# Shift and scale in three parts, and the order of the first sums, at the start of a pool and state-space decoder layer

## The chip, the cores and the metric

The kernel runs on one core of a Trainium2 chip. A core has a matrix engine (TensorE, PE in the profile), a vector engine (VectorE, DVE), a scalar engine with activation functions (ScalarE, ACT), a general engine (GpSimd, POOL), a queue engine that issues most transfers (SyncE, SP), and 16 DMA engines that move data between the chip's memory (HBM) and the core's two on-chip memories: SBUF, 128 partitions wide, and PSUM, into which PE writes.

The metric is the time of one execution on the device in microseconds (us), smaller is better. Of the kernel before there are three timed runs and one profiled execution, whose trace gives the start, the duration and the waits of every instruction.

## The reference

One layer for 1,024 prompt tokens and 64 sample tokens (8 sequences of 8), so 1,088 columns in all, with 1,024 features. Cut to what matters here:

```python
mod = jax.nn.silu(c) @ w_ada + b_ada
shift, scale, gate = jnp.split(mod, 3, axis=-1)
h = rmsnorm(x, norm_g) * (1 + scale[:, None]) + shift[:, None]
proj = h @ w_in
u_pool, z_pool, z_ssm, xbc, dt_raw, g_raw = jnp.split(proj, SPLITS, axis=-1)
...
dt = jax.nn.softplus(dt_raw + dt_bias)
...
gates = jax.nn.sigmoid(g_raw)
m = gates[..., :D_MODEL] * p + gates[..., D_MODEL:] * s
x = x + gate[:, None] * (m @ w_o)
```

`c` has nine rows: one for the prompt, eight for the samples. So shift, scale and gate are nine rows of 1,024 numbers each, made with a 1,024 x 3,072 matrix. All is in 32-bit floats.

## The kernel before

All products are made of two halves of the numbers: `hi`, which PE takes at its fast rate, and `lo`, the rest (number minus `hi`). A product is three matmuls: high by high, low by high, high by low. Activations stand with the features on the partitions, in eight blocks of 128 called k. Most of the later products with `w_in` are done two output blocks at a time by a scheme with seven products in place of eight (`strassen`, L561-623), which needs sums and differences of the four quarters of h (`combine`, L440-488) and of the weights (`first_steps`, L516).

The change lies in `first()` (L819-972), which begins the program. Its instructions are held in the order in which they are written, on each engine (`in_line`, L300); what follows is ordered by a scheduler. Its steps:

- `x_load`, `x_square`, `x_root`, `x_unit` (L207-211): nine blocks of 128 tokens (the ninth has 64) are loaded, their root mean square is made, and each is divided by it. Blocks 5 and 6 are scaled on POOL, the others on DVE.
- `x_turn(g, k)` (L215-228): PE turns feature block k of token group g (256, 384 and 448 tokens: x-blocks 0-1, 2-4, 5-8) by transposes, then a copy to `tf[k]`, for even k on DVE and for odd k on ACT.
- `ada_load`, `ada_mm`, `ada_end` (L235-259): the columns of `w_ada` for shift and scale in two parts of half the features each, eight loads of 512 KB a part. A step `ada_mm(part, k)` has four matmuls of 256 columns, each into its own 32 partitions of one PSUM bank. `ada_end` copies the bank on ACT (`mr`, L249), turns it back with two transposes (L252) and makes `md`, the scale and shift by feature, with three operations on DVE (L256, L259, L256).
- `h_make(g, ks)` (L269-295): for each k, ACT makes the high half straight from `tf` (L283, for the group with samples L292), ACT (odd k) or DVE (even k) makes h itself in place (L285, L287), and DVE the low half by subtraction (L275). Only k with `md` ready can be done, so the first half of the features comes first.
- `w_load`, `w_split` (L825 and below): the weights of two output blocks of `g_raw`, 256 KB for each half of the features, are loaded and split into `whi` (ACT, L160) and `wlo` (POOL or, where asked, DVE, L163).
- `products(g, ks)` (L837-850): these weights by h, six matmuls for each k and token group. `done` (L854-858) applies the sigmoid on ACT and stores it.
- `dt_block` (L691): the 32 columns of dt. Its activation (L701) writes into a buffer that earlier sigmoids used and that must have been stored.
- `gate_load`, `gate_mm` (L800), `gate_end` (L813): the third part of `mod`.
- `combine()` is a generator; each `next(sums)` does one portion. The first four portions are for k = 0, 1, 2 and 3: three additions or subtractions on DVE (L466-468) over half of the tokens (544 columns), the high half of `S2` on ACT (L469) and, one k behind, its low half on DVE (L462). The next portion makes `S3` (ACT L446, DVE L447, four times), then come `S1` (a subtraction, L481, high and low) and the last operand. Here `next` is called four times up to the opening and up to five times in it.
- `next(wst)` does one portion of the differences and splits of the weights of the seven products.
- `late_loads()` (L332-347) loads small constants; its second portion copies `dx` (L342, DVE) and turns two tiles on PE (L344, L345) and copies the results (L346, L347). The opening's products stand behind L345 in PE's order.
- the opening, `run(wz, hook)`: the seven products of the first two output blocks of z, 24 matmuls of 272 columns each. `hook(n)` is called behind product n and does portions of the weights (`wst`) and of the sums.

The calls ahead of the opening:

Of the kernel before, what the change touches and what calls it, by code (L numbers as in the profile page):

```python
# [8 lines left out]
F32 = mybir.dt.float32  # L9
F32R = mybir.dt.float32r  # L10
AF = mybir.ActivationFunctionType
ALU = mybir.AluOpType
# [8 lines left out]
P = 128  # L21
D = 1024
KT = D // P
# [23 lines left out]
def tile_pool_ssd_step(  # L47
# [6 lines left out]
    nc = tc.nc  # L54
# [25 lines left out]
    hp = open_("hp", 8)  # L80
# [6 lines left out]
    def G(shape=(P, T), dt=F32):  # L87
        return hp.tile(list(shape), dt, tag="G", name=nm("G"), bufs=8)
# [4 lines left out]
    def Y4(pool, dt=F32R):  # L93
        return pool.tile([P, 4, T], dt, tag="Y", name=nm("Y"), bufs=2)
# [87 lines left out]
    xr = []  # L182
# [24 lines left out]
    def x_unit(a, b):  # L207
        n = xr[a][1]
        V.reciprocal(rs[:n, a:b], rs[:n, a:b])
        for i in range(a, b):  # L210
            (nc.gpsimd if i in (5, 6) else V).tensor_scalar(xr[i][0][:n], xr[i][0][:n], rs[:n, i:i + 1], None, ALU.mult)

    tf = [None] * KT

    def x_turn(g3, k, eng=None):  # L215
        if g3 == 0:
            tf[k] = tfp.tile([P, T], F32, tag="tf", name=nm("tf"), bufs=8)
        px = PB()
        c = 0
        for i in range((0, *XG)[g3], XG[g3]):  # L220
            xt, n = xr[i]
            nc.tensor.transpose(px[:, c:c + n], xt[:n, k * P:(k + 1) * P], ident[:n, :n])
# [8 lines left out]
    pm, wraw = [None] * 2, {}  # L231
    wbig = [Y4(hp, F32), Y4(hp, F32)]
    md = const([P, 16, 9], "md")

    def ada_load(part, k):  # L235
        w = wbig[k // 4][:, k % 4, :D] if part == 0 else G((P, D))
        wraw[part, k] = w.rearrange("p (s c) -> p s c", s=2)
        load(wraw[part, k], w_ada[0, k * P:(k + 1) * P, 0:2 * D].rearrange("p (s h c) -> p s h c", s=2, h=2)[:, :, part])

    def ada_mm(part, k):  # L240
        if k == 0:
            pm[part] = PB()
        for j in range(4):
            mm(pm[part][32 * j:32 * j + 32, :256], scT[:, k, :], wraw[part, k][:, j // 2, j % 2 * 256:j % 2 * 256 + 256],
               start=(k == 0), stop=(k == KT - 1))

    def ada_end(part):
        mr = pa.tile([P, 256], F32, tag="rawA", name=nm("mr"), bufs=3)
        act(mr, pm[part][:, :256], AF.Copy)  # L249
        ps = PB()  # L250
        for i in range(2):
            nc.tensor.transpose(ps[:, i * P:(i + 1) * P], mr[:, i * P:(i + 1) * P], ident)  # L252
        pv = ps[:, :256].rearrange("p (i j b) -> p j i b", i=2, j=4)
        for s in (1, 0):
            m4 = slice(8 * s + 4 * part, 8 * s + 4 * part + 4)
            V.tensor_tensor(md[:, m4].rearrange("p (j i) b -> p j i b", i=2), pv[:, 2 * s:2 * s + 2, :, 0:9],  # L256
                            vT[:, m4].rearrange("p (j i) -> p j i", i=2).unsqueeze(3).to_broadcast([P, 2, 2, 9]), ALU.add)
            if s:
                V.tensor_tensor(md[:, m4], md[:, m4],  # L259
                                vT[:, 16 + 4 * part:20 + 4 * part].unsqueeze(2).to_broadcast([P, 4, 9]), ALU.mult)  # L260

    hb = []

# [68 lines left out]
    def late_loads():  # L332
        va = sm.tile([120, P], F32, tag="stc", name="va", bufs=4)
        load(va[0:96, :], conv_w[0].rearrange("k (m p) -> (k m) p", p=P))
        load(va[96:120, :], conv_b[0].rearrange("(m p) -> m p", p=P))
        V.memset(dtb, 0.0)
        load(dtb[0:NH, 0:1], dt_bias[0].rearrange("(h o) -> h o", o=1))
        dk = sm.tile([16, 2], F32, tag="rsm", name="dk")
        load(dk, d_skip[0].rearrange("(m h) -> m h", h=2))
        yield  # L340
        dx = sm.tile([16, 2, 64], F32, tag="stc", name="dx", bufs=4)
        V.tensor_copy(dx, dk.unsqueeze(2).to_broadcast([16, 2, 64]))  # L342
        ps = PB()
        nc.tensor.transpose(ps[:, :120], va, ident[:120, :120])  # L344
        nc.tensor.transpose(ps[:, 120:136], dx.rearrange("m h r -> m (h r)"), ident[:16, :16])  # L345
        V.tensor_copy(cvT, ps[:, :120])  # L346
        V.tensor_copy(Dv, ps[:, 120:136])  # L347
# [471 lines left out]
    def first():  # L819
# [34 lines left out]
        def done(bi, t):  # L854
            o, n = BLK[bi]
            buf = pa.tile([P, HF], F32, tag=next(tags), name=nm("g0"))
            act(buf[:, :n], banks[bi, t], AF.Sigmoid)
            store_(gs_d[t][:, o:o + n], buf[:, :n])
# [1029 lines left out]
```

## Time and profile before

| | us |
|---|---|
| timed runs: median (lowest to highest) | 1302.08 (1297.84 to 1302.78) |
| the profiled execution, its own time | 1303.16 |
| its span, first to last instruction | 1301.4 |
| mean granted clock of PE in it, share of full speed | 0.99 |
| first product (L848) starts | 39.65 |
| second half of h (k 4 to 7) starts on ACT | 57.25 |
| opening's first product (L568) starts | 84.24 |

A row of the profile names the engine, the line of the kernel, the operation, `out<-in` by the program's names, the shape and the count. Brackets at the end give the time that the engine was idle ahead of it and what ended that. In sums by stretch, each engine's busy time and count is followed by PEclk, the clock that PE was granted (1.00 is full), the busy share of the DMA engines (which can show a little over 1), and GB/s.

### The profile page before, as it was taken

What the parts mean: (1) busy time and instruction counts of PE and PEld (TensorE: products, weight loads), DVE (VectorE), ACT (ScalarE), POOL (GpSimd) and SP (SyncE); (2) the same over time, 40 slices, a digit from 0 to 9 for tenths busy, and PEclk for the clock granted to TensorE, in tenths of its full rate; (3) what the DMA queues carried; (4) which work ended last, traced back from release to release, by engine and by line L of the source; (5) the groups of instructions that cost most, each with busy time, mean ns of one, the idle gap of its engine ahead of it and who ended that gap; (6) DMA issues with size and microseconds to landing.
All of it is one profiled execution on the core that took longest, in us unless ns stands there. A gap on an engine that the chain in (4) does not pass through costs nothing.

```text
span 1301.4 us, 26116 instructions
## 1 busy us (share of the span) xinstructions
PE 1260.4 (97%) x9603; PEld 1162.7 (89%) x9603; DVE 888.8 (68%) x1507; ACT 698.3 (54%) x1659; POOL 681.0 (52%) x564
## 2 busy tenths in 40 slices
PE   5999999999999999999999999999999999999998
PEld 3778999999999999998889899888889888999786
DVE  4677579966979588775757665477666777476433
ACT  4665347465656654545555554676887866201211
POOL 2005659778869776664344453366676646214000
PEclk8999999999999999999999999999999999999999
DMA  9735445465456554444546465999998665475631
GB/s 325 231 127 177 149 147 175 149 198 188 138 168 211 157 169 133 160 134 128 166 145 196 148 176 166 351 361 372 296 280 279 210 187 163 164 273 158 228 103 51
DMA packets 231616, 251.66 MB, mean 193 GB/s; under 512 B 31137, under 2 KB 173681, under 8 KB 231482
## 3 DMA queue, kind: packets, MB, share of 16 engines
q1 hardware_dynamic: 159392, 171.59, 41.6%
q10 hardware_dynamic: 72098, 78.41, 17.7%
q8 instruction: 76, 1.25, 0.4%
q14 instruction: 50, 0.41, 0.1%
HBM read 167.06 MB, written 83.01 MB: 192 GB/s over the span
## 4 chain that ended last, share of the span: by engine, by line
PE 54%; issue 8%; POOL 5%; DMA 5%; DVE 4%; ACT 3%; SPq 0%; ACTq 0%; POOLq 0%; DVEq 0%
PE ps L568 5%; PE ps L569 5%; PE ps L570 5%; PE mm L568 5%; PE mm L570 5%; PE mm L569 5%; PE mm L320 3%; PE mm L321 3%; PE mm L322 3%; PE ps L1834 2%; PE ps L1835 2%; PE ps L1836 2%; PE ps L1160 1%; POOL G L1743 1%; PE ps L1376 1%
## 5 line engine op out<-in xcount | busy, mean ns | idle before, releaser
L163 POOL TENSOR_TENSOR wlo<-rawA,whi 128x512 fp32r<-128x512 f32 x120 | 184.0, 1538 | 188.8 <-ACT whi L160 108.1
L163 POOL TENSOR_TENSOR wlo<-raw,whi 128x512 fp32r<-128x512 f32 x92 | 149.9, 1636 | 103.7 <-ACT whi L160 98.0
L320 PE MATMUL mm<-Y,whi 128*128 128x352 f32 (+1 forms) x480 | 163.8, 341 | 0.7 <-DVE G L1737 0.6
L321 PE MATMUL mm<-Y,whi 128*128 128x352 f32 (+1 forms) x480 | 157.9, 329 | 1.0 <-DVE Y L1411 1.0
L322 PE MATMUL mm<-Y,wlo 128*128 128x352 f32 (+1 forms) x480 | 157.2, 328 | 0.0
L568 PE MATMUL mm<-Y,whi 128*128 128x272 f32 x496 | 146.4, 295 | 0.7 <-DVE u L579 0.4
L568 PE MATMUL ps<-Y,whi 128*128 128x272 f32 x496 | 144.5, 291 | 1.5 <-ACT o L768 0.8
L570 PE MATMUL mm<-Y,wlo 128*128 128x272 f32 x496 | 143.1, 289 | 2.1 <-POOL wlo L163 2.1
L569 PE MATMUL mm<-Y,whi 128*128 128x272 f32 x496 | 143.1, 289 | 0.4 <-DVE Y L447 0.4
L569 PE MATMUL ps<-Y,whi 128*128 128x272 f32 x496 | 143.1, 289 | 0.0
L570 PE MATMUL ps<-Y,wlo 128*128 128x272 f32 x496 | 142.7, 288 | 0.0
L1003 DVE SCALAR_TENSOR_TENSOR GA<-GA,cvT,GA 128x1112 f32<-128x1112 f32 x72 | 128.4, 1787 | 0.1
L160 ACT ACTIVATE whi<-rawA 128x512 fp32r<-128x512 f32 x125 | 78.1, 626 | 93.1 <-PE ps L569 38.5
L160 ACT ACTIVATE whi<-raw 128x512 fp32r<-128x512 f32 x96 | 58.8, 626 | 86.7 <-DVE raw L514 43.2
L320 PEld LDWEIGHTS mm<-Y,whi 128*128 128x128 f32 x480 | 90.7, 189 | 6.5 <-issue 3.8
L570 PEld LDWEIGHTS mm<-Y,wlo 128*128 128x128 f32 x496 | 93.4, 188 | 3.0 <-POOL wlo L163 2.7
L568 PEld LDWEIGHTS ps<-Y,whi 128*128 128x128 f32 x496 | 93.4, 188 | 3.0 <-ACT o L768 1.0
L568 PEld LDWEIGHTS mm<-Y,whi 128*128 128x128 f32 x496 | 93.3, 188 | 2.8 <-issue 0.8
L569 PEld LDWEIGHTS mm<-Y,whi 128*128 128x128 f32 x496 | 93.4, 188 | 1.5 <-DVE Y L447 0.8
L569 PEld LDWEIGHTS ps<-Y,whi 128*128 128x128 f32 x496 | 93.3, 188 | 0.4 <-issue 0.2
L570 PEld LDWEIGHTS ps<-Y,wlo 128*128 128x128 f32 x496 | 93.4, 188 | 0.2 <-issue 0.2
L321 PEld LDWEIGHTS mm<-Y,whi 128*128 128x128 f32 x480 | 90.7, 189 | 1.7 <-DVE Y L1411 1.6
(446 smaller groups left out, 3789.0 us busy)
## 6 DMA issues: line engine op xcount, KB each, us to landing
rawA<-in_w_in SPq DMA_DIRECT2D x46, 512.0 KB
dec<-acs_d SPq DMA_DIRECT2D x32, 512.0 KB
xbc<-GA ACTq DMA_DIRECT2D x24, 512.0 KB
xb<-xbc SPq DMA_DIRECT2D x32, 384.0 KB
rawA<-in_w_in SPq DMA_DIRECT2D x32, 256.0 KB
pw<-in_w_ssm_out ACTq DMA_DIRECT2D x32, 256.0 KB
ws<-ph ACTq DMA_DIRECT2D x32, 256.0 KB
ws<-pw SPq DMA_DIRECT2D x32, 256.0 KB
```

Source lines behind the costliest of these rows:

```text
L160: ins = act(hi[:, :, :ncols], raw[:, :, :ncols], AF.Copy)
L163: (eng or nc.gpsimd).tensor_tensor(lo[:, :, :ncols], raw[:, :, :ncols], hi[:, :, :ncols].bitcast(F32), ALU.subtract)
L320: mm(ps[:, :n], a, rh[k][:, o:o + n], start=(k == 0), stop=False)
L321: mm(ps[:, :n], a, rl[k][:, o:o + n], start=False, stop=False)
L322: mm(ps[:, :n], b, rh[k][:, o:o + n], start=False, stop=(k == nk - 1))
L568: mm(p, hi, ah, start=(k == 0), stop=False)
L569: mm(p, hi, al, start=False, stop=False)
L570: mm(p, lo, ah, start=False, stop=(k == 3))
L1003: V.scalar_tensor_tensor(d[:, :n], rp[:, k:k + n], cvT[:, 24 * k + mc:24 * k + mc + 1], d[:, :n], ALU.mult, ALU.add)
L1834: mm(ps[:, :cw], mhk, wo[k][0][:, s], start=(k == 0), stop=False)
L1835: mm(ps[:, :cw], mhk, wo[k][1][:, s], start=False, stop=False)
L1836: mm(ps[:, :cw], mlk, wo[k][0][:, s], start=False, stop=(k == 7))
```

## The change

`first()` and its helpers are changed in five ways:

1. Block 5 is scaled on DVE and block 6 on ACT. The turns (2,4) and (2,5) are both copied on ACT.
2. Shift and scale are made in three parts: k 0-1, k 2-3 and k 4-7. A load of the first two parts has 256 KB, its step four matmuls of 128 columns; the last part is as each part was before. Copy, transposes and the three operations are done once a part (`ada_out`, `ada_end`).
3. h and products follow in three rounds: k 0-1, 2-3, 4-7. The turns (2,6) and (2,7) come behind the first products. The loads for the second half of the weights of g, the last four loads of shift and scale and the first portion of `late_loads` are issued behind the second part's steps.
4. The first three portions of `combine` stand between the sigmoids, two sigmoids and a portion for each token group; then two dt blocks, the portion with the fourth sum, the first splits of weights, the third dt block, and the portion that makes `S3`; the second portion of `late_loads` follows that.
5. In the opening, portions of the sums are done behind products 0, 1, 3 and 4, of the weights behind 0, 2, 3 and 4.

```diff
         for i in range(a, b):
-            (nc.gpsimd if i in (5, 6) else V).tensor_scalar(xr[i][0][:n], xr[i][0][:n], rs[:n, i:i + 1], None, ALU.mult)
+            xt = xr[i][0][:n]
+            if i == 6:
+                act(xt, xt, AF.Copy, scale=rs[:n, i:i + 1])
+            else:
+                V.tensor_scalar(xt, xt, rs[:n, i:i + 1], None, ALU.mult)
...
-        if eng is not V and k % 2:
+        if eng is not V and (eng or k % 2):
...
+    PARTS = ((0, 2), (2, 4), (4, 8))
...
     def ada_load(part, k):
-        w = wbig[k // 4][:, k % 4, :D] if part == 0 else G((P, D))
-        wraw[part, k] = w.rearrange("p (s c) -> p s c", s=2)
-        load(wraw[part, k], w_ada[0, k * P:(k + 1) * P, 0:2 * D].rearrange("p (s h c) -> p s h c", s=2, h=2)[:, :, part])
+        a, b = PARTS[part]
+        w = (b - a) * P
+        if part == 0:
+            if k == 0:
+                wtile[0] = Y4(hp, F32)
+            t = wtile[0][:, k // 2, k % 2 * 512:k % 2 * 512 + 2 * w]
+        elif part == 1:
+            if k % 2 == 0:
+                wtile[1, k // 2] = G((P, D))
+            t = wtile[1, k // 2][:, k % 2 * 512:k % 2 * 512 + 2 * w]
+        else:
+            t = G((P, D))
+        wraw[part, k] = t.rearrange("p (s c) -> p s c", s=2)
+        load(wraw[part, k], w_ada[0, k * P:(k + 1) * P, 0:2 * D].rearrange("p (s c) -> p s c", s=2)[:, :, a * P:b * P])
...
     def ada_mm(part, k):
+        a, b = PARTS[part]
+        n = (b - a) * P // 2
...
-            mm(pm[part][32 * j:32 * j + 32, :256], scT[:, k, :], wraw[part, k][:, j // 2, j % 2 * 256:j % 2 * 256 + 256],
+            mm(pm[part][32 * j:32 * j + 32, :n], scT[:, k, :], wraw[part, k][:, j // 2, j % 2 * n:j % 2 * n + n],
...
+    def ada_out(part):
+        a, b = PARTS[part]
+        n = (b - a) * P // 2
         mr = pa.tile([P, 256], F32, tag="rawA", name=nm("mr"), bufs=3)
-        act(mr, pm[part][:, :256], AF.Copy)
+        act(mr[:, :n], pm[part][:, :n], AF.Copy)
+        return mr
...
         for k in range(KT):
-            if k == 2:
-                w_load(0, 1)
-                w_load(1, 1)
             ada_load(1, k)
+        for k in range(4):
+            ada_load(2, k)
         late = late_loads()
-        next(late)
...
-        ada_mm(0, 0)
         for k in range(4):
-            x_turn(2, k)
-            if k % 2:
-                ada_mm(0, 1 + k // 2)
+            ada_mm(0, k)
+        x_turn(2, 0)
+        x_turn(2, 1)
+        ada_mm(0, 4)
+        ada_mm(0, 5)
         w_split(0, 0)
         w_split(1, 0)
-        ada_mm(0, 3)
-        x_turn(2, 4)
-        ada_mm(0, 4)
-        x_turn(2, 5)
-        ada_mm(0, 5)
+        x_turn(2, 2)
+        x_turn(2, 3)
         ada_mm(0, 6)
         ada_mm(0, 7)
+        mr = ada_out(0)
+        x_turn(2, 4, nc.scalar)
+        x_turn(2, 5, nc.scalar)
+        ada_end(0, mr)
+
+        h_make(0, range(2))
+        products(0, range(2))
         x_turn(2, 6)
-        ada_end(0)
-
-        h_make(0, range(4))
         x_turn(2, 7)
-        products(0, range(4))
-        h_make(1, range(4))
-        ada_mm(1, 0)
-        ada_mm(1, 1)
+        h_make(1, range(2))
+        products(1, range(2))
+        h_make(2, range(2))
+        for k in range(KT):
+            ada_mm(1, k)
+        w_load(0, 1)
+        w_load(1, 1)
+        for k in range(4, 8):
+            ada_load(2, k)
+        next(late)
+        mr = ada_out(1)
+        products(2, range(1))
+        ada_end(1, mr)
+        products(2, range(1, 2))
+
+        for bi in range(2):
+            h_make(bi, range(2, 4))
+            products(bi, range(2, 4))
+        h_make(2, range(2, 4))
         w_split(0, 1, V)
         w_split(1, 1, V)
-        products(1, range(4))
-        h_make(2, range(4))
-        for k in range(2, 8):
-            ada_mm(1, k)
-        products(2, range(2))
+        for k in range(4):
+            ada_mm(2, k)
+        products(2, range(2, 3))
+        for k in range(4, 8):
+            ada_mm(2, k)
+        mr = ada_out(2)
+        products(2, range(3, 4))
...
         next(wst)
-        ada_end(1)
-        products(2, range(2, 4))
+        ada_end(2, mr)
...
+        sums = combine()
+        for bi in range(3):
+            done(bi, 0)
+            done(bi, 1)
+            next(sums)
+        dt_block(dtw, 0)
+        dt_block(dtw, 1)
+        next(sums)
         next(wst)
-        for bi in range(3):
-            for t in range(2):
-                done(bi, t)
-        sums = combine()
-        for i in range(3):
-            dt_block(dtw, i)
-            next(sums)
+        dt_block(dtw, 2)
+        next(sums)
         for k in range(4, 8):
             gate_mm(k)
         next(late, None)
-        next(sums)
         gate_end(bg)
-        next(wst)

         def hook(n):
-            if 0 < n < 4:
+            if n in (0, 2):
                 next(wst)
-            if n < 5:
+            if n < 2:
+                next(sums)
+            if n in (3, 4):
+                next(wst)
                 next(sums)
         run(wz, hook)
```

More of the change, by code (lines that the diff above doesn't have):

```diff
@@ L228, in x_turn @@
             V.tensor_copy(tf[k][:, o:o + c], px[:, :c])
-    pm, wraw = [None] * 2, {}
-    wbig = [Y4(hp, F32), Y4(hp, F32)]
+    PARTS = ((0, 2), (2, 4), (4, 8))
+    pm, wraw, wtile = [None] * 3, {}, {}
     md = const([P, 16, 9], "md")
     def ada_load(part, k):
-        w = wbig[k // 4][:, k % 4, :D] if part == 0 else G((P, D))
-        wraw[part, k] = w.rearrange("p (s c) -> p s c", s=2)
-        load(wraw[part, k], w_ada[0, k * P:(k + 1) * P, 0:2 * D].rearrange("p (s h c) -> p s h c", s=2, h=2)[:, :, part])
+        a, b = PARTS[part]
[12 more added lines that the diff above has]
+        load(wraw[part, k], w_ada[0, k * P:(k + 1) * P, 0:2 * D].rearrange("p (s c) -> p s c", s=2)[:, :, a * P:b * P])
     def ada_mm(part, k):
+        a, b = PARTS[part]
+        n = (b - a) * P // 2
         if k == 0:
@@ L243, in ada_mm, with ada_end @@
         for j in range(4):
-            mm(pm[part][32 * j:32 * j + 32, :256], scT[:, k, :], wraw[part, k][:, j // 2, j % 2 * 256:j % 2 * 256 + 256],
+            mm(pm[part][32 * j:32 * j + 32, :n], scT[:, k, :], wraw[part, k][:, j // 2, j % 2 * n:j % 2 * n + n],
                start=(k == 0), stop=(k == KT - 1))
-    def ada_end(part):
+    def ada_out(part):
+        a, b = PARTS[part]
+        n = (b - a) * P // 2
         mr = pa.tile([P, 256], F32, tag="rawA", name=nm("mr"), bufs=3)
-        act(mr, pm[part][:, :256], AF.Copy)
+        act(mr[:, :n], pm[part][:, :n], AF.Copy)
+        return mr
+    def ada_end(part, mr):
+        a, b = PARTS[part]
+        ni = (b - a) // 2
         ps = PB()
-        for i in range(2):
+        for i in range(ni):
             nc.tensor.transpose(ps[:, i * P:(i + 1) * P], mr[:, i * P:(i + 1) * P], ident)
-        pv = ps[:, :256].rearrange("p (i j b) -> p j i b", i=2, j=4)
+        pv = ps[:, :ni * P].rearrange("p (i j b) -> p j i b", i=ni, j=4)
         for s in (1, 0):
-            m4 = slice(8 * s + 4 * part, 8 * s + 4 * part + 4)
-            V.tensor_tensor(md[:, m4].rearrange("p (j i) b -> p j i b", i=2), pv[:, 2 * s:2 * s + 2, :, 0:9],
-                            vT[:, m4].rearrange("p (j i) -> p j i", i=2).unsqueeze(3).to_broadcast([P, 2, 2, 9]), ALU.add)
+            m = slice(8 * s + a, 8 * s + b)
+            V.tensor_tensor(md[:, m].rearrange("p (j i) b -> p j i b", i=ni), pv[:, 2 * s:2 * s + 2, :, 0:9],
+                            vT[:, m].rearrange("p (j i) -> p j i", i=ni).unsqueeze(3).to_broadcast([P, 2, ni, 9]), ALU.add)
             if s:
-                V.tensor_tensor(md[:, m4], md[:, m4],
-                                vT[:, 16 + 4 * part:20 + 4 * part].unsqueeze(2).to_broadcast([P, 4, 9]), ALU.mult)
+                V.tensor_tensor(md[:, m], md[:, m],
+                                vT[:, 16 + a:16 + b].unsqueeze(2).to_broadcast([P, b - a, 9]), ALU.mult)
     hb = []
```

## The prediction

> **What bounds the kernel now.** I read the page first, then the sums over two stretches of the span (windows: busy time of each engine, granted PE clock, share of the DMA engines, GB/s), and then went through the first stretch with the timeline of each engine and the waits of PE.
>
> ```profile
> span 1301.4 us, 26116 instructions
> PE 1260.4 (97%) x9603; PEld 1162.7 (89%) x9603; DVE 888.8 (68%) x1507; ACT 698.3 (54%) x1659; POOL 681.0 (52%) x564
> 0.00:112.00 112.00, 92.96 (x713) 72.07 (x713) 75.49 (x154) 64.02 (x117) 15.79 (x36) 0.92 0.64 212
> 112.00:1301.40 1189.40, 1167.41 (x8893) 1090.64 (x8891) 813.36 (x1354) 634.31 (x1543) 665.16 (x528) 1.00 0.59 192
> 20.00:30.00 10.00, 5.69 (x30) 2.79 (x31) 3.42 (x8) 1.50 (x4) 5.37 (x2) 0.58 1.07 367
> ```
>
> PE sets the end. After 112 us it is busy for 1167.41 of 1189.40 us at full clock. Nothing there changes its order, so what is gained or lost before 112 us is carried to the end about one for one. Before that PE is idle for 19 us and the granted clock averages 0.92: that is all the change can work on. Three places matter: the wait on GpSimd's two blocks, the chain from the last shift/scale matmul to the first product, and the wait ahead of the opening.
>
> ```profile
> 19.15 6.22 POOL L211 TENSOR_SCALAR Y<-Y,rs 128x1024 f32<-128x1024 f32 x2 [15.78 <-DVE rs L209]
> PE ps L222 <- POOL Y L211: 3.9, 2, 2.3
> 20.40 0.64 PE L244 MATMUL ps<-Y,scT 128*32 128x256 f32 x8 [1.06 <-issue]
> 26.34 0.90 PE L222 MATMUL ps<-ident,Y 128*128 128x128 f32 x3
> 27.46 1.08 PE L244 MATMUL ps<-Y,scT 128*32 128x256 f32 x8
> 28.48 0.90 PE L222 MATMUL ps<-ident,Y 128*128 128x128 f32 x3
> 37.24 0.38 ACT L249 ACTIVATE mr<-ps 128x256 f32<-128x256 f32 x1 [0.92 <-PE ps L244]
> 39.65 0.39 PE L848 MATMUL mm<-Y,whi 128*128 128x256 f32 x1 [0.89 <-ACT Y L283]
> ```
>
> In the timeline rows stand start, duration, engine, line and operation, then the idle time before it and what ended it; in the waits row us in total, times, longest. A turn of the last blocks costs PE 1.12 us (26.34 to 27.46), one step of shift/scale 1.02 (27.46 to 28.48). The sums are in at 37.24, when their copy starts; the first product follows 2.4 us later, behind copy, transpose, three vector operations and h.
>
> **1. The start: first product some 7 us earlier.** Blocks 5 and 6 go to DVE and ACT, so PE's 3.9 us of waiting on POOL goes; no row shows such a scaling there, but POOL's 3.1 us each is the ceiling, and it runs beside the steps. Before, PE came to its first step at 20.4. Now eight steps of half the columns (half of 1.02, 4.1 us) and four turns (4.5) stand between that point and the sums, since two turns are put behind them: sums in at 29.0, the first product 2.4 us later, 31.4; with the two turns that now lie in that chain on PE and ACT, at 32 to 33. The loads don't gate this: the quarter is 2.1 MB instead of 4.2, at 367 GB/s 5.7 us less, and even before, the waits on PE hold none for them.
>
> **2. The middle: given back.** What was left out comes behind the first product: two turns (2.2 us at that clock, 1.1 at full) and the second quarter, whose eight steps of half width cost 2 to 4.1 us. So 3.1 to 6.3 of the 7 us are only moved.
>
> ```profile
> 40.89 0.28 PE L849 MATMUL mm<-Y,wlo 128*128 128x256 f32 x1
> 41.01 0.28 PE L850 MATMUL mm<-Y,whi 128*128 128x256 f32 x1
> 42.37 0.42 PE L848 MATMUL mm<-Y,whi 128*128 128x256 f32 x1
> 42.58 0.41 PE L849 MATMUL mm<-Y,wlo 128*128 128x256 f32 x1
> 57.25 1.09 ACT L283 ACTIVATE G<-tf,md 128x256 fp32r<-128x256 f32 x2 [2.98 <-DVE md L256]
> ```
>
> The rest goes to a third serial round. A 256-column matmul takes 0.12 us at full clock (40.89 to 41.01) and 0.21 at half (42.37 to 42.58). Six of them per k (a block of 128 features) make 0.72 us of products for the first token block, by columns 1.08 for the second and 1.26 for the third. A round "sums in, copy, transpose, add, h, first product" lasts 2.4 us. In round two its cover is the third token block's two k, 2.5 us, but the copy and the three adds (a 0.38 us copy as at 37.24, and vector operations) stand in ACT's and DVE's queues behind the wide last h. Per k, h costs ACT and DVE 12.5/4 = 3.1 us (57.25 to 69.77, where DVE's last low waits for ACT's last high, below) and PE's products 3.06, so neither runs ahead of the other. Forward from 32.5: 6.1 us for products of two k, at a mixed clock about 8; second quarter and turns 4; the chain less its cover plus queueing, about 1: 45.5. Then 6.1 of products, 3.8 for eight steps at full width and clock (four matmuls of 0.12 each), 1.5 to 2 of waits on h: 57, where before the second half's h starts at 57.25. I take a gain of 0.2 us; bounds are -3.9 (all that isn't moved is kept) and +3 (as many half-clock stretches as in 5).
>
> The second pair of gate weights is loaded behind the second quarter's matmuls on SP, and behind it the last four loads of the shift/scale weights: 0.5 MB and 4x0.5 MB at 367 GB/s are 6.8 us from about 43, in at about 50, when PE wants the fifth step at about 52. I take nothing, and 1.5 us as a rival. The small late loads and the memset go back on SP and DVE too, but are wanted only at 78 and 83: nothing, 40 us hide them.
>
> **3. Ahead of the opening: +3.8 us.** From the end of h DVE works through this:
>
> ```profile
> 69.77 0.63 DVE L275 TENSOR_TENSOR G<-tf,G 128x448 fp32r<-128x448 f32 x1 [0.39 <-ACT G L292]
> 70.31 1.29 DVE L163 TENSOR_TENSOR wlo<-rawA,whi 128x512 fp32r<-128x512 f32 x2
> 72.24 0.72 DVE L466 TENSOR_TENSOR tf<-tf,tf 128x544 f32<-128x544 f32 x1
> 75.91 0.72 DVE L468 TENSOR_TENSOR tf<-tf,tf 128x544 f32<-128x544 f32 x1
> 79.77 0.73 DVE L462 TENSOR_TENSOR Y<-tf,Y 128x544 fp32r<-128x544 f32 x1 [3.14 <-ACT Y L469]
> 80.42 0.72 DVE L466 TENSOR_TENSOR tf<-tf,tf 128x544 f32<-128x544 f32 x1
> 89.77 2.63 DVE L447 TENSOR_TENSOR Y<-tf,Y 128x544 fp32r<-128x544 f32 x4
> 82.95 0.32 PE L344 MATMUL ps<-ident,va 120*128 120x120 f32 x1
> 84.08 0.23 PE L345 MATMUL ps<-ident,dx 16*128 16x16 f32 x1 [0.81 <-DVE dx L342]
> ```
>
> PE's last step before the opening is the transpose of dx (L345), whose copy DVE makes in its written order. PE is there at 83.27 (the row at 82.95 ends) and waits 0.81 us. Now all four first sums, their lows, the split and the difference and the four lows of S3 stand ahead of dx; before, the fourth sum, two lows and the four of S3 came behind it. DVE alone: 12 adds at 0.73 (72.24 to 75.91 is five steps), 4 lows at 0.65 (79.77 to 80.42), the split and difference 1.93 (70.31 to 72.24), 2.63 for S3: 15.9 us from 70.4 is 86.3, dx at 86.5. The 3.14 us that DVE waited for ACT's high half behind six sigmoids is what the interleaving removes; without that DVE would need 19.
>
> ACT may be later than that:
>
> ```profile
> 69.64 1.14 ACT L160 ACTIVATE whi<-rawA 128x512 fp32r<-128x512 f32 x2
> 70.80 1.28 ACT L857 ACT_TABLE_LOAD   x1
> 72.09 0.39 ACT L857 ACTIVATE g<-mm 128x256 f32<-128x256 f32 x1
> 78.21 0.47 ACT L701 ACTIVATE dts<-mm,dtb 128x256 f32<-128x256 f32 x1 [1.06 <-DMA gs<-g]
> 79.08 0.66 ACT L469 ACTIVATE Y<-tf 128x544 fp32r<-128x544 f32 x1 [0.40 <-ACT dts L701]
> 81.50 0.58 ACT L701 ACTIVATE dts<-mm,dtb 128x384 f32<-128x384 f32 x1 [1.76 <-DMA gs<-g]
> 89.06 2.31 ACT L446 ACTIVATE Y<-tf 128x544 fp32r<-128x544 f32 x4
> ```
>
> The second dt block writes the buffer of the last sigmoid and waits for its store to land (81.50). Three high halves now stand between the sigmoids (3x0.66), the two splits (1.14) have gone from their front, so the store is issued 0.9 us later. Behind its landing in ACT's order: the dt block 0.58 and its store, 0.4 (78.21 to 79.08 less 0.47), S2's fourth high 0.66, the splits 1.14, the third dt block 1.0, S3's four highs 2.31: from 82.4 that is 88.5; DVE's last low and dx, 0.9: 89.4. So dx is ready between 86.5 (DVE alone sets it) and 89.4 (the store's landing does). I take 87.9, the middle, because that landing is the one time I can't place: opening at 88.0 against 84.24, +3.8, bounds +2.4 and +5.3. PE, there at 83.3, idles for more than 4 us.
>
> **4. In the opening: -1.7 us.**
>
> ```profile
> PE mm L569 <- DVE S L447: 0.6, 1, 0.6
> PE mm L569 <- DVE Y L447: 0.4, 1, 0.4
> PE mm L569 <- DVE R L447: 0.4, 1, 0.4
> PE mm L568 <- DVE s L579: 0.3, 1, 0.3
> L570 PE MATMUL mm<-Y,wlo 128*128 128x272 f32 x496 | 143.1, 289 | 2.1 <-POOL wlo L163 2.1
> ```
>
> With S3 done ahead, DVE has 6.4 us less to do there (three adds, two lows, S3's four), so these four waits, 1.7 us, go. Bounds: -1.4 (the last is another kind) and -2.5 (each restart costs some tenths more). The weight splits move the other way: the third and fourth go from ahead of the opening to behind its first product, the rest one product later. The nearest stall on a split is 2.1 us in the whole program; I put 0.7 here and at the start of the next group, bounds 0 and 2.1.
>
> **5. The clock.** In 20 to 30 us, where PE is 57% busy, the granted clock is 0.58; and a half-clock stretch is 3.41 us long:
>
> ```profile
> 42.14:45.55 3.41, 3.41 (x16) 3.33 (x16) 1.86 (x5) 3.38 (x7) 0.00 (x0) 0.50 1.10 339
> ```
>
> One more costs a busy PE half of that, 1.7 us. The idle stretch at the opening may bring one: +0.8, bounds 0 and +5.1 (three, if the chopped middle brings them too).
>
> The Trainium skill, "TensorE: Matmul & The Clock Gate", section "Why this matters for your kernels", says that idle gaps of over about 3 us between matmuls send TensorE back to half clock. By that rule the gap ahead of the opening is sure to cost its 1.7 us. The 2.3 us gap before 25.4 us lies in the stretch with 0.58, which agrees, but this start has other gaps beside it; no trace here shows a long gap after dense work.
>
> **Sum** against the profiled 1303.16 us (span 1301.4 and 1.8 around it): -0.2 + 3.8 - 1.7 + 0.7 + 0.8 = +3.4. The profiled execution lies 1.1 above the median of the runs, 1302.08, and I take the median: **1305.5 us**.
>
> **Rivals.** *The chopped start keeps the clock low* (slower). Three short rounds with waits on h leave PE idle in many small pieces between 30 and 58 us; the gap ahead of the opening adds one. For it: the 0.58 row, and a half-clock stretch at 42 with only two half-microsecond waits before it. Against: from 45.55 on the clock holds through dense work. Price: two half-clock stretches more than I counted and the bound of +5.3 ahead of the opening: 3.4 + 2x1.7 + 1.5 = +8.3, 1310.4; it decides as soon as two stretches beyond the present ones fall between 33 and 90 us. *The early start is kept* (faster). Cover suffices in both rounds: the second half starts at 53.4 instead of 57.25, DVE's chain, the sigmoids and their stores come as much earlier, dx with them: -3.9 + 2.4 - 2.5 = -4.0, with no splits or clock to pay: 1298.1. For it: products and h cost the same per feature, so one round hides another; against: the queueing above. *The loads arrive late* and take the place of POOL's wait: the second quarter and the last half wait for free buffers, 1.5 us, +4.9: 1307.0. *It doesn't do what it says*: DVE and ACT are through with the sums before PE comes to dx, and the opening's waits come back from other work; then +3.8 and -1.7 both fall away: +1.3, 1303.4. The chain at 69.77 to 86.3 speaks against it.
>
> **Numbers.** Forecast 0.48, low clock 0.24, kept start 0.14, late loads 0.08, no effect 0.06. Below 0.5% (6.5 us) a measurement of this kernel doesn't tell a change from none. Slower by more: most of the low clock (0.22) and the tail of the forecast (0.03), 0.25. Faster by more would need 1295.6, beyond the kept start's 1298.1, by perhaps half of its cases: 0.07. Same: 0.68. Range 1297 to 1311.5: from a little below the kept start to a little above the low clock.
>
> **What would show it.** Right: first product at 32 to 33; second half's h at 56 to 58; no wait on POOL's units; a wait of 3 to 6 us on dx at L345; the waits on the lows (L447) gone. Wrong: second half's h before 55 (kept start) or after 59; granted clock below 1.00 between 80 and 95; waits on L238's loads in the middle; a dx wait under 2 us.

## The result, and the profile after

The changed kernel took 1310.46 us in the median of five runs (1305.49 to 1312.58), the kernel before 1300.65 beside it: ratio 1.007, 95% interval 1.004 to 1.0099. Timed again, with twelve runs, it was 1309.63 against 1303.51: ratio 1.005 (1.003 to 1.007). So it is 0.5 to 0.7% slower, 6.5 to 9 us, where +3.4 us was forecast; the median lies within the stated range, the increase is 2 to 2.6 times the forecast.

Both parts of the change show in the traces: the three-part start (points 1 to 3) and the new order of the sums (points 4 and 5). First the start, in the timelines of PE and ACT (columns as before) of the changed kernel, whose line numbers are 24 higher from `h_make` on:

```profile
28.89 0.38 PE L872 MATMUL mm<-Y,whi 128*128 128x256 f32 x1 [1.20 <-ACT Y L307]
55.17 1.09 ACT L307 ACTIVATE G<-tf,md 128x256 fp32r<-128x256 f32 x2 [1.78 <-DVE md L280]
```

The first product comes 10.8 us earlier than before (39.65), the second half's h only 2.1 us earlier (57.25): 26.3 us lie between them in place of 17.6. The waits of PE from 18 to 120 us show both where that goes and what comes after it:

```profile
PE ps L369 <- DVE dx L366: 3.6, 1, 3.6
PE mm L872 <- ACT Y L307: 2.4, 2, 1.2
PE ps L261 <- issue: 1.6, 1, 1.6
PE mm L874 <- DVE Y L299: 1.3, 3, 0.5
PE mm L872 <- ACT G L307: 1.3, 1, 1.3
PE mm L592 <- ACT whi L160: 1.1, 2, 0.8
PE mm L874 <- DVE G L299: 0.9, 2, 0.5
PE mm L594 <- DVE wlo L163: 0.5, 1, 0.5
```

POOL's scaling is gone from the list, and so are the opening's four waits on lows and sums (L447, now L471, and L579). In their place stand the copy of dx, the weight splits, and longer waits on h's highs and lows: 5.9 us in three rounds (2.4 + 1.3 + 1.3 + 0.9), where the kernel before has 2.1 in two:

```profile
PE mm L850 <- DVE Y L275: 0.9, 2, 0.5
PE mm L848 <- ACT Y L283: 0.9, 1, 0.9
PE mm L850 <- DVE G L275: 0.3, 1, 0.3
```

In DVE's and PE's timelines of the changed kernel, the last low of h, DVE's only wait between it and dx, then dx and the opening:

```profile
67.67 0.63 DVE L299 TENSOR_TENSOR G<-tf,G 128x448 fp32r<-128x448 f32 x1 [0.39 <-ACT G L316]
79.33 0.73 DVE L486 TENSOR_TENSOR Y<-tf,Y 128x544 fp32r<-128x544 f32 x1 [0.50 <-ACT Y L493]
84.50 0.21 DVE L366 COPY dx<-dk 16x128 f32<-16x128 f32 x1
84.76 0.29 PE L369 MATMUL ps<-ident,dx 16*128 16x16 f32 x1 [3.58 <-DVE dx L366]
84.98 0.60 PE L592 MATMUL mm<-Y,whi 128*128 128x272 f32 x1
90.41 0.29 PE L592 MATMUL mm<-G,whi 128*128 128x272 f32 x1
```

The opening's first product, 24 matmuls, takes 5.43 us (84.98 to 90.41), and at the pitch of 0.127 us that the other products have it would take 3.05. The sums by stretch say why; the second and third rows are of another execution of the same kernel:

```profile
83.35:90.18 6.83, 5.42 (x24) 5.38 (x25) 2.05 (x6) 0.60 (x2) 0.00 (x0) 0.50 0.05 11
```

```profile
20.00:35.00 15.00, 13.46 (x98) 8.99 (x99) 4.73 (x14) 6.65 (x15) 2.74 (x3) 0.50 1.09 355
84.00:100.00 16.00, 12.56 (x118) 11.29 (x111) 11.20 (x21) 9.54 (x18) 0.00 (x0) 1.00 0.09 32
```

In the first profile the clock is half for 6.83 us around the opening, and was full from 20 to 35 us. In the second it is half all through 20 to 35, so that the first product comes at 32.56 and the opening at 89.90, and full behind the wait. Half-clock stretches fall differently in each execution, and one profile shows one of the draws (the last section works out a part of why).

A mark behind the opening tells the progress of each kernel: the first small memset of 15 columns in a GA tile on DVE (L732), which comes at the same place of the program in all.

| | ratio to before (95%) | median us | before beside it | first product | second half's h | opening | mark |
|---|---|---|---|---|---|---|---|
| before | | 1302.08 | | 39.65 | 57.25 | 84.24 | 142.40 |
| changed | 1.007 (1.004 to 1.0099) | 1310.46 | 1300.65 | 28.89 | 55.17 | 84.98 | 143.39 |
| changed, again | 1.005 (1.003 to 1.007) | 1309.63 | 1303.51 | 32.56 | 60.27 | 89.90 | 145.39 |
| early dx | 1.0011 (0.9995 to 1.0027) | 1305.68 | 1303.82 | 28.12 | 55.78 | 81.89 | 137.76 |
| three parts, old sums | 1.0023 (1.0006 to 1.004) | 1307.57 | 1303.82 | 29.23 | 56.48 | 84.07 | 141.84 |
| before, scaling alone | 0.9991 (0.997 to 1.0012) | 1302.89 | 1303.80 | 32.34 | 49.26 | 76.08 | 135.76 |
| two parts, scaling, new sums, early dx | 0.9933 (0.9908 to 0.9958) | 1295.51 | 1303.80 | 35.40 | 52.80 | 78.91 | 135.34 |

The last four are kernels of the experiments. Ratios and medians are of timed runs, the four times behind them of the one profile that goes with the row. Ratios are what compares, since the groups ran on different chips, each beside the kernel before.

### The profile page after: what moved, and what is told of

Its sections match the earlier page's. It is cut to its first block, busy times and chain, and to the rows that moved or that the text cites. A ratio compares the mean times of both kernels' runs of the same rounds, so it can differ in the third digit from the quotient of the medians.

```text
span 1305.6 us, 26257 instructions
## 1 busy us (share of the span) xinstructions
PE 1260.7 (97%) x9667; PEld 1164.8 (89%) x9667; DVE 887.2 (68%) x1510; ACT 700.6 (54%) x1662; POOL 677.9 (52%) x562
## 3 DMA queue, kind: packets, MB, share of 16 engines
q10 hardware_dynamic: 72098, 78.41, 17.6%
## 4 chain that ended last, share of the span: by engine, by line
PE 79%; DVE 6%; DMA 6%; ACT 3%; issue 3%; POOL 2%; ACTq 0%; SPq 0%; DVEq 0%; POOLq 0%
PE ps L592 8%; PE mm L592 7%; PE ps L593 7%; PE ps L594 7%; PE mm L594 7%; PE mm L593 7%; PE mm L344 5%; PE mm L345 4%; PE mm L346 4%; PE ps L1878 2%; PE ps L1879 2%; PE ps L1880 2%; PE ps L1204 2%; PE ps L1420 1%; PE ps L1207 1%
## 5 line engine op out<-in xcount | busy, mean ns | idle before, releaser
L163 POOL TENSOR_TENSOR wlo<-rawA,whi 128x512 fp32r<-128x512 f32 x120 | 187.0, 1563 | 198.2 <-ACT whi L160 104.6
```

The costliest lines, as they stand in the source:

```text
L163: (eng or nc.gpsimd).tensor_tensor(lo[:, :, :ncols], raw[:, :, :ncols], hi[:, :, :ncols].bitcast(F32), ALU.subtract)
```

## The experiments

**The early dx.** One DVE instruction is moved.

```diff
         V.tensor_copy(dx, dk.unsqueeze(2).to_broadcast([16, 2, 64]))
+        yield
...
+        next(late)
         sums = combine()
```

> The changed kernel with one DVE instruction moved: the copy of dx stands ahead of the first sum and not behind S3's lows; all other orders are the same. Theory (the wait ahead of the opening and what it does to the clock): PE comes to L345's transpose at 81.2 and finds dx ready, the 3.6 us wait goes, the opening starts at about 81.5 and no half-clock stretch follows (83.4 to 90.2 in the changed kernel, some 24 matmuls at 0.23 us in place of 0.13, 2.4 us): 4 to 6 us faster than the changed kernel, 1304 to 1306, with less spread. Rival (the weight splits, now later in the opening, set its pace): the opening starts early but waits inside for wlo and whi, ends where it ended, and the time stays at 1309 to 1311.

1305.68 us, ratio 1.0011: 5 to 8 us below the changed kernel, by the two ratios of that. The wait on dx is gone, the opening starts at 81.89, and the clock behind it is full:

```profile
80.00:95.00 15.00, 14.53 (x133) 13.34 (x121) 13.42 (x25) 10.72 (x21) 0.00 (x0) 1.00 0.12 40
```

The opening's weights don't set its pace: waits on them, 0.9 and 0.5 us, are about as long as in the changed kernel. So by these medians the late copy of dx, with what it does to the clock, is worth more than half of the loss. But the mark, at 137.76, is 4.6 us ahead of before, and the end isn't.

**PE busy while it waits.** The results of these matmuls are not read.

```diff
+        warm = PB()
+        for i in range(26):
+            mm(warm[:, :SB], hh_[i % 4][:, :P], hh_[i % 4][:, :SB], start=True, stop=True)
         next(late, None)
```

> The changed kernel with 26 matmuls of 272 columns (3.3 us) that nobody reads, put on PE ahead of the transpose of the late constants, so that PE is busy while it waits for dx. Theory (the idle gap brings the half clock): the opening starts at 84.9 as in the changed kernel, but at full clock: some 2.4 us faster than the changed kernel in the opening, about 1307 to 1308, and the runs spread less. Rival (the half clock comes by itself, or costs nothing since DVE sets the opening's pace): same time as the changed kernel, 1310.

1308.24 us, ratio 1.0032 (1.0011 to 1.0053): 2 to 5 us below the changed kernel, with intervals that overlap. The opening starts at 85.36, as late as ever, but at full clock, so its first product is as fast as the others:

```profile
80.00:95.00 15.00, 14.67 (x128) 13.72 (x121) 10.97 (x21) 8.59 (x16) 0.00 (x0) 1.00 0.07 23
```

The runs didn't spread less (1302.9 to 1318.4). One profile doesn't show that the idle gap brings the half clock, since the changed kernel's second profile has full clock behind a gap of 3.4 us. All fourteen profiles together do: in the ten in which PE waits 0.8 us or less ahead of the opening, the opening runs at full clock; of the four with a wait of 2.7 us or more, three have half clock there. Its size in time, 2.4 us in the first profile, agrees with the timing but isn't separated by it.

**Three parts with the old sums**: everything from the sigmoids to the opening as before.

```diff
-        sums = combine()
+        next(wst)
         for bi in range(3):
-            done(bi, 0)
-            done(bi, 1)
+            for t in range(2):
+                done(bi, t)
+        sums = combine()
+        for i in range(3):
+            dt_block(dtw, i)
             next(sums)
...
```

> The changed kernel with everything from the sigmoids to the opening as before (sums behind the sigmoids, weight splits ahead, the old portions in the opening): only the three parts, the loads and the scaling on DVE and ACT are left of the change. Theory (the first part of the change gains, the second loses): h ends at 68.3 as in the changed kernel, 2.1 us earlier than before; the old chain of 13.4 us from there puts dx at 81.9 and the opening at about 82.2, with the old waits: 2 us faster than before, 1298 to 1300. Rival (the chopped start is what costs, by clock or later): no faster than before, 1303 or more.

1307.57 us, ratio 1.0023: slower than before, so the rival holds. The second half's h starts at 56.48, 1.3 us later than in the changed kernel's first profile, PE doesn't wait for dx, and the opening begins at 84.07 in place of the 82.2 that were expected, about where it began before the change (84.24): what was to be gained ahead of it isn't there.

**The new sums on the old start.** The second part of the change alone.

> The kernel before with only the second part of the change (first sums between the sigmoids, splits between the seven). Theory: h ends at 70.4 as before, dx follows 16.2 us later at 86.6, PE waits some 3.5 us for it and the clock falls to half for one or two stretches: 4 to 10 us slower than before. Rival (only with the early start does DVE's longer chain show): within 2 us of before.

1307.16 us, ratio 1.0017 (1.0001 to 1.0034). Its edit is the lower third of the change's diff, on the kernel before. PE waits 5.1 us for dx, and half clock follows, as a row of the waits and then the sums from 86 to 94 us show:

```profile
PE ps L345 <- DVE dx L342: 5.1, 1, 5.1
```

```profile
86.00:94.00 8.00, 5.22 (x24) 5.19 (x25) 3.42 (x8) 1.98 (x4) 0.00 (x0) 0.57 0.07 23
```

The mechanism is as expected, but the cost in time, about 2 us, is below the 4 to 10 us of the theory and at the edge of what the rival allows. A part of the difference is that the opening's own waits of before (L447, L579, 1.7 us) are not among this kernel's.

**Both kernels profiled again.**

> The kernel before, profiled once more. Theory (its rest after 150 us is the same work in the same order as in the others): the span lies within 1299 to 1307 as its timed runs do, the half-clock stretch at 21 to 35 us is there again, and the waits of PE on POOL's wlo between 140 and 1000 us are the 2.1 us of the first profile. Rival (the first profile was a favourable one behind 150 us): those waits are 4 us as in the four kernels run so far, and the span is 3 us or more above 1301.4.

> The changed kernel, profiled and timed once more beside the others. Theory: 3.6 us of waiting on dx, half clock for one or two stretches from about 83 us, 6 us behind the kernel with the early dx at 150 us; in time 4 to 6 us above that kernel (1305.7), so 1309 to 1311. Rival (the differences at 150 us don't reach the end): within 2 us of 1305.7.

The kernel before: ratio 0.9992, span 1302.1, half clock from 21.8 to 35.5 us again, waits on POOL's wlo 2.9 us, between the 2.1 of the first profile and the 4 of the rival. In span and clock its first profile was no exception. The changed kernel: 1309.63 us, as told above; PE waits 3.4 us for dx, but no half clock follows this time.

**The early dx, with PE held up 4.3 us**: 34 unread matmuls at the same place as the 26 above.

> The kernel with the early dx, and 34 matmuls of 272 columns that nobody reads (34 x 0.127 = 4.3 us) on PE ahead of the opening: everything else as there, only that the opening starts 4.3 us later, which takes back what that kernel has won at 150 us. Theory (PE sets the end, a shift before 112 us is carried one for one): 4.3 us slower than the kernel with the early dx, 1310. Rival (behind 150 us other engines' work and transfers take an early PE's lead away): within 1.5 us of it, 1305 to 1307.

1308.21 us, ratio 1.0026 (1.0002 to 1.0051), 2 us above the early dx without the hold: between the two theories, and the intervals hold both. Inconclusive.

**The kernel before, held up 4.3 us behind the opening**, with the same 34 matmuls behind `run(wz, hook)`.

> The kernel before with 34 matmuls of 272 columns (4.3 us) that nobody reads on PE right behind the opening: nothing ahead of it changes. Theory (behind the opening PE sets the end, a shift there is carried one for one): 4 to 4.5 us slower than before, 1308. Rival (the rest has waits of PE on other engines that take up a shift, as the kernel with the early dx and its held twin, 1305.7 and 1308.2, suggest): 1 to 3 us slower.

1310.02 us, ratio 1.0043 (1.0025 to 1.006): 5.6 us for 4.3, with an interval of 3.3 to 7.8. This answers what the last one left open for a shift behind the opening: it is carried to the end in full. (Its profiled execution was the fastest of twelve, so its span says nothing here.)

**The changed kernel with the blocks scaled on POOL again.**

```diff
-            xt = xr[i][0][:n]
-            if i == 6:
-                act(xt, xt, AF.Copy, scale=rs[:n, i:i + 1])
-            else:
-                V.tensor_scalar(xt, xt, rs[:n, i:i + 1], None, ALU.mult)
+            (nc.gpsimd if i in (5, 6) else V).tensor_scalar(xr[i][0][:n], xr[i][0][:n], rs[:n, i:i + 1], None, ALU.mult)
```

> The changed kernel with blocks 5 and 6 scaled on POOL again. Theory (the wait on POOL costs its 3.9 us and the clock with it): the first product comes at 34 or later in place of 28.9, the clock is half from about 22 to 35 us, h ends 3 to 5 us later than 68.3, and the end is 2 to 4 us later than the changed kernel's. Rival (the first quarter would wait elsewhere): the first product within 1.5 us of 28.9.

1316.85 us, ratio 1.0094 (1.0065 to 1.0123). The first product comes at 35.67, PE waits 3.6 us on POOL, and the opening begins at 93.69. So three parts without the faster scaling are slower still than the changed kernel, by 3 to 6 us by the two ratios (2 to 4 were expected), and the early first product is owed to the scaling about as much as to the quarter: without the scaling it comes 3.1 to 6.8 us later than in the changed kernel's two profiles, and still 4.0 us earlier than before.

**The scaling alone, on the kernel before** (that edit the other way round).

> The kernel before with one thing changed: block 5 is scaled on DVE and block 6 on ACT in place of POOL. Theory (the gain of the changed start comes from this, by the 3.9 us wait and the clock, and the three parts cost behind 150 us): first product at about 35 to 36, the half-clock stretches between 22 and 35 us shorter, 2 to 5 us faster than before, 1299 to 1301, and so 6 us or more below the kernel with three parts and the old sums (1307.6), which has this scaling too. Rival (the three parts cost nothing, something else in the rest takes an early start away): no faster than before, 1303 or more.

1302.89 us, ratio 0.9991 (0.997 to 1.0012): no difference that can be measured, though its profile has the opening at 76.08 and the mark 6.6 us ahead. That execution took 1297.72 us, one of the fastest of twelve (1294.64 to 1307.25), with one half-clock stretch before 100 us. What its start gains on average isn't told by it. Against the three parts with the same scaling and the same sums (1.0023), it is 0.3% faster, with intervals that just overlap.

**Two parts with all the rest**: the kernel before with the scaling, the new sums and the early dx.

> The kernel before with the scaling on DVE and ACT, the new order of sums and splits, and the early copy of dx: the kernel with the early dx less its three parts. Theory (three parts cost more behind 150 us than they bring): faster than the kernel with the early dx (1305.7) and than the one before, 1297 to 1301. Rival (the three parts are neutral or gain): 1305 to 1308.

1295.51 us, ratio 0.9933 (0.9908 to 0.9958): faster than both kernels, 8.7 us below before. What it lacks against the early dx kernel (1.0011) are the three parts, with the order of loads and turns that comes with them; the intervals lie well apart. Its first product is 7.3 us later than that one's, but its second half of h is 3 us earlier. Two rows of its timeline, its sums from 39.5 to 60 us, and the same stretch in the changed kernel:

```profile
35.40 0.39 PE L853 MATMUL mm<-Y,whi 128*128 128x256 f32 x1 [0.89 <-ACT Y L287]
52.80 1.09 ACT L287 ACTIVATE G<-tf,md 128x256 fp32r<-128x256 f32 x2 [2.98 <-DVE md L260]
```

```profile
39.50:60.00 20.50, 20.20 (x170) 16.68 (x170) 14.85 (x38) 14.84 (x26) 0.00 (x0) 0.97 0.70 217
```

```profile
39.50:60.00 20.50, 17.80 (x166) 13.27 (x159) 11.93 (x31) 11.79 (x22) 0.00 (x0) 1.00 0.89 294
```

With two parts PE is busy for 20.20 of 20.50 us there, and DVE and ACT for 14.8 each. With three parts PE is busy for 17.80 and DVE and ACT for 11.9 and 11.8: no engine is full, the rounds wait for each other.

**The same with other buffers.** Behind the opening the orders of the two- and three-part kernels are the same, but the latter waits more there (below). One thing that differs is which buffer of each kind comes next.

```diff
+        for t in [Y4(hp, F32)[:, 0]] + [G((P, D)) for _ in range(4)] + [PB() for _ in range(2)] + [
+                pa.tile([P, 256], F32, tag="rawA", name=nm("turned"), bufs=3)]:
+            V.memset(t[:, 0:1], 0.0)
         for i in range(9):
             x_load(i)
```

> The kernel with the scaling on DVE and ACT, the new sums and the early dx, on two parts; at its very start eight tiles are taken and one column of each is set on DVE, so that every later tile of these kinds (G, Y, rawA and the PSUM banks of the second pool) falls into the buffer that the kernel with three parts gives it. Nothing else changes, and the order on PE, ACT, POOL and SP is the same. Theory (the small waits behind 150 us that the three parts bring come from their start itself, not from which buffers the rest uses): within 2 us of the kernel without them, 1294 to 1298. Rival (other buffers, other conflicts): 3 us or more above, 1299 to 1303, with more waits on POOL's wlo behind 150 us than its 1.8 us.

1295.89 us, ratio 0.9968 (0.9949 to 0.9986): by the median as without it, by the ratio 0.35% above it with intervals that just overlap, and again faster than before. PE's wait on POOL's wlo from 140 us on, in the kernel before, the changed one, the early dx, the two-part kernel and this one:

```profile
PE mm L570 <- POOL wlo L163: 2.1, 3, 1.4
```

```profile
PE mm L594 <- POOL wlo L163: 4.4, 5, 1.6
```

```profile
PE mm L595 <- POOL wlo L163: 4.1, 5, 1.5
```

```profile
PE mm L575 <- POOL wlo L163: 1.8, 3, 1.2
```

```profile
PE mm L575 <- POOL wlo L163: 1.7, 3, 1.1
```

So the buffers are not the cause of these waits; in time, a part of the difference isn't excluded by the ratios.

## Why the prediction came out as it did

Of the signs that the prediction named, those of the second part came: no wait on POOL's scaling, 3.6 and 3.4 us of waiting on dx, no waits on the lows. Those of the start came in part: the first product at 32 to 33 in the second profile alone, the second half's h at 56 to 58 in neither (55.17 and 60.27). Two signs of being wrong came in one profile each: h after 59 in the second, and a clock below 1.00 between 80 and 95 us in the first (0.77). The direction was right and the size too low; that the time still lies in the range is partly luck, for its upper end was set for the low clock, and the excess arises behind the opening, for which the sum had no term: at the mark the two profiles are 1.0 and 3.0 us behind the kernel before, not more than the forecast.

*The start, first product at 32 to 33.* It came at 28.89 and 32.56. The sum was right for a half clock from 20 to 35 us; with POOL's wait gone the clock may be full there, and then it is 3 to 4 us earlier. The scaling alone gives 32.34 and 35.40, so the quarter itself adds some 3 to 4 us, not most of the 7.

*The middle, given back.* The forecast was 24.5 us from the first product to the second half's h; the two profiles show 26.3 and 27.7, the two-part kernels 17.4 and 16.9. This is the right mechanism, and a part of what the three parts cost: between the early dx kernel and the two-part one, 3.0 us at the second half's h and 2.4 at the mark. The step left out the comparison that mattered: it set the round trip against the kernel before, which still had POOL's wait, took -0.2 us, and so put the loss down to the second part of the change. With the scaling on DVE and ACT, the four profiles with three parts in the table have the second half's h at 55.17 to 60.27, the two with two parts at 49.26 and 52.80. In time the three parts cost 0.3% (three parts with old sums against the scaling alone) to 0.8% (early dx against two parts; 0.4% against its twin with other buffers): 4 to 10 us.

*Ahead of the opening, +3.8.* The chain was right in length: from h's end at 68.30 (67.67 + 0.63) to dx at 84.71 are 16.4 us, and 16.1 were worked out for DVE alone. The upper bound was not needed: in the profile of the changed kernel DVE waits only 0.5 us for ACT there (the row at 79.33), so the landing of the sigmoid's store didn't decide, and the middle that was taken, 17.5 us behind h's end, was 1.1 us too long. The wait of PE, 3.6 and 3.4 us, is as forecast (3 to 6).

*In the opening, -1.7 and +0.7.* The four waits are gone. The splits cost 1.1 + 0.5 us in the first profile and 0.5 + 0.5 in the second, within the bounds of 0 to 2.1. (DVE's 6.4 us less are 6.1 by the prediction's own rows; nothing hangs on it.)

*The clock, +0.8.* Undersized where it happened: two stretches in the first profile (6.83 us, 2.4 us lost in the opening), none in the second. Over the timed runs the mean clock of the changed kernel was 0.989, that of the kernel before beside it 0.990, and 0.985 with POOL's scaling. The Trainium skill, "TensorE: Matmul & The Clock Gate", section "Why this matters for your kernels", has gaps of over about 3 us end in half clock. The trace agrees for 3.58 us, and with the unread matmuls in the gap there is no such stretch; but the 3.4 us gap of the second profile had none either, and a gap of 2.7 us in another kernel had one. The Trainium skill, "TensorE: Matmul & The Clock Gate", Part 1, section "What's actually happening", says that the window over which activity is counted runs freely and doesn't begin with the kernel. The traces agree, and it fits a draw that differs with each execution (last section).

*Carried one for one.* Right for a shift as such (5.6 us for 4.3, within the interval). But the three-part kernels also lose behind 140 us, which no step had. The waits of PE from 140 to 1290 us add up to 13.0 to 16.4 us in the seven profiles with two parts, to 15.4 to 19.5 in the seven with three, 14.8 against 17.5 in the mean. Between the early dx kernel and the two-part one it is 18.3 against 13.2, and 10 us in the spans, of which 2.4 stand at the mark and 1.7 are one half-clock stretch more behind it. Single profiles overlap, and why a start with three parts makes the rest wait more stays open; the order of the instructions behind the opening is the same, and turning the buffers doesn't bring the waits (13.0 us).

The kept start, the rival on the fast side, fell for the three parts by the rounds of waits; the two-part kernel comes near its numbers (52.80 for 53.4, 1295.51 for 1298.1) by another route. The low clock, the rival on the slow side (1310.4), comes closest to the measured time, but its sign, two half-clock stretches (6.8 us) more than before between 33 and 90 us, didn't come: the two profiles have 10.2 and 7.3 us at half clock there, the kernel before 5.7. The excess of the first is in the opening, not in a chopped start, and the rest of the time arises behind the opening.

## What to carry to other kernels

Cutting a serial preparation into more parts brings the first use forward, but each part adds a round of "copy, turn, add, make, use". Here that cost more than it brought; our reading, which no run tests by itself, is that the makers (ACT and DVE) are no faster than the user, so that nothing hides a round. Compare against the kernel with the other improvements in place, not against the old one. When a reordering moves long work ahead of a short instruction that another engine waits for (the copy of dx, 0.2 us), move that instruction too: here it was worth 5 us or more and decided whether the reordered sums gained or lost. Test the parts of a change one by one and in pairs: here the best kernel takes the scaling and the new sums, moves the copy of dx, and leaves out the three parts.

## What was not expected of the hardware

The same kernel had the clock at 1.00 in one execution and at 0.50 in another through the whole of 20 to 35 us, which moved its first product by 3.7 us. Gaps of PE ahead of the opening of 5.1, 3.6, 3.4 and 2.7 us were followed by two, two, no and one half-clock stretch of 3.41 us, the last in the kernel with POOL's scaling:

```profile
PE ps L365 <- DVE dx L362: 2.7, 1, 2.7
```

```profile
90.00:100.00 10.00, 7.31 (x52) 6.68 (x45) 4.65 (x11) 4.16 (x9) 0.00 (x0) 0.83 0.10 32
```

What decides is not the length of the gap alone. In each of the fourteen traces the half-clock stretches begin a whole number of 3.413 us apart (in the changed kernel at 35.56, 83.35 and 673.86 us, 14 and 173 times that), and this raster lies elsewhere in each execution. Here are the windows of the raster that hold the gap, in the changed kernel, its second profile (two windows) and the kernel with POOL's scaling:

```profile
79.94:83.35 3.41, 1.24 (x21) 0.47 (x13) 3.38 (x7) 3.01 (x6) 0.00 (x0) 1.00 0.20 71
```

```profile
84.68:88.10 3.42, 1.62 (x29) 0.68 (x20) 3.38 (x6) 3.02 (x7) 0.00 (x0) 1.00 0.20 71
88.10:91.51 3.41, 1.77 (x13) 1.75 (x14) 2.28 (x7) 0.44 (x1) 0.00 (x0) 1.00 0.02 6
```

```profile
90.79:94.20 3.41, 0.72 (x6) 0.65 (x6) 3.09 (x8) 1.53 (x3) 0.00 (x0) 1.00 0.11 38
```

In the first and the last PE is idle for 2.2 and 2.7 us of one window, and half clock follows. In the second profile the raster cuts the gap in two, 1.8 and 1.6 us, and none follows. Behind 75 us the fourteen traces have 20 windows in which PE is idle for 2.0 us or more, and half clock follows each; between 1.85 and 2.0 us it follows some. With less than 1.85 us a change from full to half clock comes five times, all between 1148 and 1160 us behind windows without idle time, so idle time isn't the whole rule.

So with a start of this kind two profiles of one kernel differ by 5 us at the opening and by 2 us at the mark, and only ratios of many runs tell what a change is worth.
